# Gated attention's pieces spread over its blocks, the first loads on two queues, and the last normalization shared by VectorE and TensorE

## The chip, the cores and the metric

The kernel runs on one core of a Trainium2 chip. The metric is the device time of one execution in microseconds (us); a kernel is run several times and the median is compared. Everything below is about the five engines of that core: PE (TensorE, matmuls), DVE (VectorE), ACT (ScalarE), POOL (GpSimd) and SP (SyncE, which here only issues transfers), and about the core's 16 DMA engines.

## What is computed

One decoder layer over 256 tokens of 2048 features, in float32. Cut to what matters:

```
u = x @ W_in                                   # blocks cg, ca, v, qk, r, cq, ck, cv, sc, sh, sb of 512 columns, and g_low of 16
y_a = silu(LN(depthwise_conv31(ca * sigmoid(cg))))           # 31 taps over 256 tokens
log_a = log_sigmoid(g_low @ w_g2 + b_g2) / 16                # forget gate of the gated linear attention
y_b = rms_norm(chunked gated linear attention of q, k, v with exp(cumsum(log_a))) * silu(r)
y_c = dilated attention of cq, ck, cv;   y_d = sb * conv3(sc * sh)
x1  = LN1(alpha * x + (concat(y_a, y_b, y_c, y_d) * mix_scale) @ W_out)
acc = alpha * x1 + HierMoE(x1)                 # 32 experts, 2 for each token
      + sigmoid(x1 @ W_g + b_g) * (p @ W_p)
out = (acc - mean) * rstd * ln2_g + ln2_b      # LN2, the last normalization
```

## The kernel before

**Projections.** Each block of W_in is a [2048 x 512] weight that arrives in two halves of 8 row tiles (`k`). A call of `proj_ch` or `proj_tok` walks over the 16 `k`: ACT casts the weight tile to a rounded copy (`wh`, L252), DVE or POOL subtracts it from the original for the rest (`wl`, L255; every third tile goes to POOL), and PE multiplies three times: high by high, low by high, high by low (L275 to L277). That makes 12 matmuls of 256 columns for one `k`. Four pairs of `wh` and `wl` exist, so the split can run at most four tiles ahead of PE.

**The first block.** `first_half` loads weight and input in turn; `load_x` issues the transfer of some tiles of x, casts them (`xh`, L204) and subtracts (`xl`, L205). The first tile of x comes over SP's queue, the other eight transfers over POOL's; the weights `cgw` all come over SP's.

**The pieces.** After each `k` the projection calls `pump(rate)`. It runs `rate` pieces of work from the list `tasks` (generators, each piece up to a `yield`), and when `tasks` is empty from `behind`, which holds the 31-tap convolution `conv` of block A (DVE: 4 x 30 multiply-adds at L334). `gla_gate` (the forget gate) is the task under block `qk`, `gla_state` (the chunked state, 7 steps of four DVE updates between matmuls) under block `r`, `gla_out` under `cq`. `drain()` finishes what is left of `tasks`. On top of this order in the program, a scheduler of the framework orders the instructions of each engine, so the order in the program and that on an engine are not the same.

**Experts.** After routing, `group` runs ten groups of experts. Their weights stream over SP's queue into five slots; four expert units share the PE array in strips of 32 columns (L1101, L1144), and `scatter` adds the results to `acc` (L1161 to L1166). A spill-over path for overfull experts sits in a branch (`tc.If(flag > 0)`), not taken here; `flag` is computed on DVE (`ov`) and loaded into a register on every engine (L1214).

**The last normalization.** `norm_stats` (L665 to L673) gives mean, `rstd` and `-mean * rstd` for each token. The 256 x 2048 result is eight pieces of 128 x 512 (`rows(acc, t, db)`). Two of them (i = 1 and 4) go over ACT (L1229) and two POOL operations (L1230, L1231), six over two DVE operations each (L1237, L1239); each piece is written out by one transfer on SP's queue.

Of the kernel before, what the change touches and what calls it, by code (L numbers as in the profile page):

```python
# [19 lines left out]
P = 128  # L20
T = 256
# [103 lines left out]
def trunk(ctx, tc, where, vecs_d, lasting, early, gla, xT, x, pT_d, w_in, w_out, ple_w_gate, exp_w_gu, exp_w_down, ple_w_proj, out):  # L125
# [74 lines left out]
    xl = bx.tile([P, KT, T], F32R, name="xl", tag="xb")  # L200

    def load_x(ks):
        (nc.gpsimd if ks.start else nc.sync).dma_start(xin[:, ks], xT[:, ks])
        S.copy(xh[:, ks], xin[:, ks])  # L204
        V.tensor_sub(xl[:, ks], xin[:, ks], f32(xh[:, ks]))  # L205

# [4 lines left out]
    def quarter(q, part, shape=None, name="mix"):  # L211
        return qm.tile(shape or [P, 4, T], F32 if shape else F32R, name=name, tag=f"q{q}{part}")
# [21 lines left out]
    def drain():  # L234
        while tasks:
            pump()

    def load_half(w, name, sizes=(4, 4), before=None):

        s = slot([P, 8, 512], name)  # L240
        a = 0
        for n in sizes:
            if before is not None:
                before(a, a + n)
            nc.sync.dma_start(s[:, a:a + n], w[:, a:a + n])
            a += n
        return s
# [8 lines left out]
        return wh, wl  # L256

    def first_half(k, w, name):
        s = load_half(w, name, (2, 2, 2, 2) if k else (1, 1, 2, 2, 2), lambda a, b: load_x(slice(k + a, k + b)))
        if k:  # L260
            small_loads()
        return s
# [51 lines left out]
    wgl = const("wgl", t=at_g).rearrange("p (k c) -> p k c", k=KT)

    b = bank("gl")
    for k in range(KT):
        o = 32 * (k % 4)
        PE.matmul(b[o:o + 32, :T], wgl[:, k, :], xin[:, k, :], start=k < 4, stop=k >= KT - 4, skip_group_check=True,
                  tile_position=(0, o))  # L320
    glT = quarter(3, "l", [P, T], "glT")
    V.tensor_copy(glT, b[:, :T])
# [59 lines left out]
    behind.append(conv())  # L382


    vb = proj_tok(w_in[list(BLOCKS).index("v")], "v", lambda k: xh[:, k], lambda k: xl[:, k])
    vv = work([P, 2, 512], name="vv")
    for t in range(NT):
# [44 lines left out]
        yield  # L432

    tasks.append(gla_gate())
    us = proj_ch("qk")
    drain()
    qq = work([P, 2, 2, T], name="qq")
    kk = work([P, 2, 2, T], name="kk")
    for blk in range(2):
        V.scalar_tensor_tensor(qq[:, 0, blk, :], us[blk], 0.125, e12[:, 0, blk, :], op0=ALU.mult, op1=ALU.mult)  # L440
        V.scalar_tensor_tensor(qq[:, 1, blk, :], us[blk], 0.125, e34[:, 0, blk, :], op0=ALU.mult, op1=ALU.mult)
        V.tensor_mul(kk[:, 0, blk, :], us[2 + blk], e12[:, 1, blk, :])
        V.tensor_mul(kk[:, 1, blk, :], us[2 + blk], e34[:, 1, blk, :])

    ob = []

    def gla_state():
        kd = work([P, 2, 256], name="kd")
        state = work([P, 2, 2, 256], name="state")
        G.memset(state, 0.0)  # L450
# [52 lines left out]
            yield  # L503

    tasks.append(gla_state())
    rb = proj_ch("r")
    drain()
    sr = work([P, 4, T], name="sr")
    cg = cp.tile([P, 4], F32, name="cg")
# [45 lines left out]
    q_ = work([P, 4, T], name="q_")  # L555
    for cb in range(4):
        S.activation(q_[:, cb, :], backwards(cq[cb]), AF.Copy, scale=0.125)
    ck = proj_ch("ck")
    k_ = work([P, 4, T], name="k_")
    for cb in range(4):  # L560
        S.copy(k_[:, cb, :], ck[cb])
    cv = proj_tok(w_in[list(BLOCKS).index("cv")], "cv", lambda k: xh[:, k], lambda k: xl[:, k])
    v_ = work([P, 2, 512], name="v_")
    for t in range(NT):
        S.copy(v_[:, t, :], cv[t])
# [437 lines left out]
    def slots_and_gates():  # L1003
        for src, dst in ((sg4, sB), (gt.rearrange("p c t o -> p (c t o)"), gB)):
# [203 lines left out]
    ov = stage([1, 34], F32, name="ov")
    V.tensor_copy(ov[:, 0:32], orders[:, 32:64])
    V.tensor_sub(ov[:, 0:32], ov[:, 0:32], const("tab", 1)[:, 32:64])  # L1210
    V.reduce_max(ov[:, 32:33], ov[:, 0:32], axis=AX.X)
    V.tensor_scalar(ov[:, 32:33], ov[:, 32:33], 0.0, 1.0, op0=ALU.max, op1=ALU.min)
    V.tensor_copy(orders[:, 64:65], ov[:, 32:33])
    flag = nc.values_load(orders[0:1, 64:65], min_val=0, max_val=1, skip_runtime_bounds_check_because="0 or 1")  # L1214
# [5 lines left out]


    S.activation(agg[:, 8], eps_ln, AF.Sqrt)
    with tc.manual_schedule(engines={ET.DVE, ET.Pool, ET.Activation}):
        ms = norm_stats(4)
        for i in range(8):
            t, db = i % 2, i // 2
            if i in (1, 4):
                av = rows(acc, t, db)
                S.activation(av, av, AF.Identity, scale=ms[t][1], bias=ms[t][2])  # L1229
                G.tensor_mul(av, av, rows(gbB, 0, db))  # L1230
                G.tensor_add(av, av, rows(gbB, 1, db))  # L1231
                nc.sync.dma_start(out[t * P:(t + 1) * P, db * 512:(db + 1) * 512], av)
        todo = [i for i in range(8) if i not in (1, 4)]
        for js in ([0, 1], [2, 3], [4, 5]):
            part = [(rows(acc, i % 2, i // 2), i % 2, i // 2) for i in (todo[j] for j in js)]
            for av, t, db in part:
                V.scalar_tensor_tensor(av, av, ms[t][0], rows(gbB, 0, db), op0=ALU.subtract, op1=ALU.mult)  # L1237
            for av, t, db in part:
                V.scalar_tensor_tensor(av, av, ms[t][1], rows(gbB, 1, db), op0=ALU.mult, op1=ALU.add)  # L1239
                nc.sync.dma_start(out[t * P:(t + 1) * P, db * 512:(db + 1) * 512], av)  # L1240


# [22 lines left out]
```

## Time and profile before

| | |
|---|---|
| median of 3 runs | 958.7 us (956.8 to 960.71) |
| the profiled execution: its own time | 958.87 us |
| its span in the trace | 957.0 us |
| PE busy | 897.9 us (94% of the span) |
| DVE busy | 448.8 us (47%) |
| ACT busy | 294.9 us (31%) |
| POOL busy | 137.6 us (14%) |
| mean granted clock of PE | 0.983 of full speed |

The span is the time from the first to the last instruction; the execution's own time is 1.9 us longer. "Busy" of an engine is an average over stages in which different things end last, so it does not say what a change in one stage is worth. The stages are, roughly: the first block to 40 us, the other projections to 400 us, routing to 440 us, the experts to 936 us, and the last normalization.

### The profile page before, as it was taken

Reading aid. Unit: us, or ns where it says so; the run is one execution under the profiler, and the core shown is the slowest. Engines: PE = TensorE matmul, PEld = TensorE weight load, DVE = VectorE, ACT = ScalarE, POOL = GpSimd, SP = SyncE. Lnnn points to the kernel's source line nnn. Section 1 sums busy time; section 2 is a strip of 40 time slices with the busy share of each in tenths; the row PEclk is TensorE's granted clock in tenths of the full one; section 3 lists DMA queues with packets and bytes.
Section 4 is the critical chain, followed back from the end, with each engine's and each line's share of the span. In section 5 each row is a group of like instructions: output and inputs, shape, how many; then the busy total and the mean of one; then the engine's idle time right before and its main releaser. Section 6 shows DMA issues by size and latency. Waiting matters only on the chain. (4 is left out here: it accounts for less than half of the span.)

```text
span 957.0 us, 14896 instructions
## 1 busy us (share of the span) xinstructions
PE 897.9 (94%) x5542; PEld 546.9 (57%) x5542; DVE 448.8 (47%) x902; ACT 294.9 (31%) x537; POOL 137.6 (14%) x124
## 2 busy tenths in 40 slices
PE   8998899999999999989999989999999999998981
PEld 7897887998989888944333353234533342441220
DVE  4469999746558554563351051032403253340327
ACT  5444523557554544551110121011202121120012
POOL 3233322322322332200000000000000000000002
PEclk9999999999999999989999999999999999999996
DMA  9954422654444754329999999999999999999972
GB/s 343 420 194 175 164 102 94 222 188 158 177 177 174 252 196 176 132 80 351 385 369 409 403 400 410 401 407 416 407 407 396 415 417 417 409 407 394 338 269 90
DMA packets 75855, 280.88 MB, mean 293 GB/s; under 512 B 7000, under 2 KB 7136, under 8 KB 63744
## 3 DMA queue, kind: packets, MB, share of 16 engines
q1 hardware_dynamic: 72256, 267.40, 72.9%
q0 software_dynamic: 3520, 12.47, 3.3%
q8 instruction: 45, 0.74, 0.3%
q14 instruction: 34, 0.28, 0.1%
HBM read 290.31 MB, written 2.11 MB: 306 GB/s over the span
## 5 line engine op out<-in xcount | busy, mean ns | idle before, releaser
L1101 PE MATMUL gu<-we,xg 128*32 128x512 f32 x1184 | 157.7, 597 | 8.3 <-DMA we<-in_exp_w_gu_dram 8.3
L746 PE MATMUL pl<-plw,x1T 128*128 128x512 f32 x256 | 124.3, 618 | 0.0
L1101 PEld LDWEIGHTS gu<-we,xg 128*32 128x32 f32 x1184 | 37.6, 109 | 109.1 <-issue 74.5
L1144 PE MATMUL y<-wd,hT 128*32 128x512 f32 x624 | 84.8, 605 | 6.6 <-DMA wd<-in_exp_w_down_dram 3.6
L1126 DVE SCALAR_TENSOR_TENSOR h<-h,gw,gu 128x256 f32<-128x256 f32 x10 | 4.8, 482 | 180.7 <-ACT h L1125 180.7
L1164 DVE TENSOR_TENSOR xn<-xn,sc 128x512 f32<-128x512 f32 x76 | 50.5, 684 | 79.4 <-PE sc L1162 79.4
L746 PEld LDWEIGHTS pl<-plw,x1T 128*128 128x128 f32 x256 | 46.3, 193 | 67.7 <-issue 66.2
L1125 ACT ACTIVATE h<-gu 128x256 f32<-128x256 f32 x10 | 3.8, 384 | 220.1 <-PE gu L1101 220.1
L334 DVE SCALAR_TENSOR_TENSOR ya<-hp,ce,ya 128x255 f32<-128x255 f32 (+29 forms) x120 | 65.0, 587 | 0.2
L252 ACT CAST wh<-wow 128x512 fp32r<-128x512 f32 (+1 forms) x80 | 42.8, 535 | 46.6 <-PE wo L295 32.7
L1148 ACT CAST yh<-y 128x512 fp32r<-128x512 f32 x40 | 23.4, 586 | 106.0 <-PE sc L1161 60.0
L295 PE MATMUL wo<-wh,mix 128*128 128x512 f32 (+1 forms) x160 | 54.1, 347 | 0.0
L294 PE MATMUL wo<-wh,mix 128*128 128x512 f32 (+1 forms) x160 | 54.1, 347 | 0.0
L255 DVE TENSOR_TENSOR wl<-wow,wh 128x512 fp32r<-128x512 f32 (+1 forms) x53 | 32.2, 612 | 45.5 <-ACT wh L252 42.0
L723 POOL DMA_DIRECT2D plw<-in_ple_w_gate_dram x16 | 8.6, 534 | 279.0 <-PE pl L746 175.8
L1144 PEld LDWEIGHTS y<-wd,hT 128*32 128x32 f32 x624 | 18.0, 110 | 53.4 <-issue 28.9
L965 PE MATMUL xg<-M,xnh 128*128 128x256 f32 x160 | 43.6, 307 | 5.1 <-ACT xg L970 2.7
L1149 DVE TENSOR_TENSOR yl<-y,yh 128x512 fp32r<-128x512 f32 x40 | 27.4, 686 | 39.6 <-ACT yh L1148 39.0
L296 PE MATMUL wo<-wl,mix 128*128 128x512 f32 (+1 forms) x160 | 42.6, 347 | 0.0
L970 ACT ACTIVATE xg<-xg,cl 128x256 f32<-128x256 f32 x40 | 22.5, 564 | 59.5 <-DVE xg L973 59.5
L965 PE MATMUL xg<-M,xnl 128*128 128x256 f32 x160 | 39.9, 283 | 0.0
L965 PEld LDWEIGHTS xg<-M,xnh 128*128 128x128 f32 x160 | 30.4, 190 | 14.7 <-ACT xg L970 6.0
(481 smaller groups left out, 1942.2 us busy)
## 6 DMA issues: line engine op xcount, KB each, us to landing
we<-in_exp_w_gu_dram SPq DMA_DIRECT2D x168, 512.0 KB, 10.2
wd<-in_exp_w_down_dram SPq DMA_DIRECT2D x92, 512.0 KB, 10.8
we<-in_exp_w_gu_dram SPq DMA_DIRECT2D x32, 1024.0 KB, 15.8
wow<-in_w_out_dram SPq DMA_DIRECT2D x16, 1024.0 KB, 7.2
wd<-in_exp_w_down_dram SPq DMA_DIRECT2D x16, 1024.0 KB, 17.1
wd<-in_exp_w_gu_dram SPq DMA_DIRECT2D x24, 512.0 KB, 6.2
plw<-in_ple_w_gate_dram POOLq DMA_DIRECT2D x16, 512.0 KB, 7.0
plw<-in_ple_w_gate_dram SPq DMA_DIRECT2D x6, 1024.0 KB, 6.4
```

Source lines behind the costliest of these rows:

```text
L252: S.copy(wh, w)
L255: e.tensor_sub(wl, w, f32(wh))
L294: PE.matmul(o, lh(k)[:, ts], wh, start=i == 0, stop=False)
L295: PE.matmul(o, ll(k)[:, ts], wh, start=False, stop=False)
L296: PE.matmul(o, lh(k)[:, ts], wl, start=False, stop=i == KT - 1)
L334: V.scalar_tensor_tensor(ya[:, cb, d:T], hp[:, cb, 0:T - d], dww(30 - d, cb), ya[:, cb, d:T], op0=ALU.mult, op1=ALU.add)
L746: PE.matmul(bs[t], x1T[:, k, t * P:(t + 1) * P], s, start=False, stop=k == KT - 1, skip_group_check=True)
L965: PE.matmul(o, part[:, t, (k0 + j) * P:(k0 + j + 1) * P], m_[:, t, :], start=j + t + i == 0, stop=t + i == 2, skip_group_check=True)
L1101: PE.matmul(gu[us, :], xg[:, k0 + k, xo + us.start:xo + us.stop], s[:, q, k, :], start=k0 + k == 0, stop=k0 + k == KT - 1, skip_group_chec ...
L1144: PE.matmul(y[us, :], hT[:, k, us], s[:, q, k, c0:c0 + 512], start=k == 0, stop=k == 1, skip_group_check=True, tile_position=(0, us.start))
L1149: V.tensor_sub(yl, y, f32(yh))
L1164: V.tensor_add(rows(acc, t, db), rows(acc, t, db), o)
```

## The change

1. **First loads.** The first two tiles of x are issued by ACT, the rest by SP; POOL issues none. The pieces are larger: weights of the first half in 1, 1, 2 and 4 tiles (before 1, 1, 2, 2, 2), of the second half in 4 and 4 (before four of 2).
2. **Pieces.** The small projection of `g_low` (`wgl`, 16 matmuls) stands behind block `ca` and the start of the convolution instead of ahead of `ca`. The rates of `pump` become 0.6 under `qk`, 1.15 under `r`, and 1.25 under `ck` and `cv` (before 1 each). The eight operations that make `qq` and `kk` move from a block of their own into the first two pieces of `gla_state`.
3. **Flag.** `ov` is computed right after routing, and the flag is loaded before the last expert group.
4. **Last normalization.** POOL is out. DVE subtracts the mean and multiplies by `ln2_g` in all eight pieces. For i = 0 to 3, PE then adds `ln2_b` (`spread`: one matmul that spreads a row over 128 partitions) and multiplies by `rstd` with a diagonal matrix `dg` (one float32 matmul of 512 columns), and ACT copies the result out of PSUM. For i = 4 to 7 DVE does the second step too.

```
     def load_x(ks):
-        (nc.gpsimd if ks.start else nc.sync).dma_start(xin[:, ks], xT[:, ks])
+        (nc.scalar if ks.stop <= 2 else nc.sync).dma_start(xin[:, ks], xT[:, ks])
...
-        s = load_half(w, name, (2, 2, 2, 2) if k else (1, 1, 2, 2, 2), lambda a, b: load_x(slice(k + a, k + b)))
+        s = load_half(w, name, (4, 4) if k else (1, 1, 2, 4), lambda a, b: load_x(slice(k + a, k + b)))
...
-    us = proj_ch("qk")
+    us = proj_ch("qk", 0.6)
     drain()
-    qq = work([P, 2, 2, T], name="qq")
...
     def gla_state():
+        qq = work([P, 2, 2, T], name="qq")
+        kk = work([P, 2, 2, T], name="kk")
+        for blk in range(2):
+            V.scalar_tensor_tensor(qq[:, 0, blk, :], us[blk], 0.125, e12[:, 0, blk, :], op0=ALU.mult, op1=ALU.mult)
...
+            yield
...
-    rb = proj_ch("r")
+    rb = proj_ch("r", 1.15)
...
+            flag = nc.values_load(orders[0:1, 64:65], min_val=0, max_val=1, skip_runtime_bounds_check_because="0 or 1")
         group(g, RT[g], last=g == NG - 1)
...
+    with tc.manual_schedule(engines={ET.PE, ET.DVE, ET.Activation}):
         ms = norm_stats(4)
+        dg = []
+        for t in range(NT):
+            dg.append(stage([P, P], F32, name="dg"))
+            S.activation(dg[t], ident, AF.Identity, scale=ms[t][1])
+
         for i in range(8):
             t, db = i % 2, i // 2
...
+            av = rows(acc, t, db)
+            V.scalar_tensor_tensor(av, av, ms[t][0], rows(gbB, 0, db), op0=ALU.subtract, op1=ALU.mult)
+            if i < 4:
+                b = bank("o", "y", 3)
+                spread(b, 16 + db, True, False)
+                PE.matmul(b, dg[t], av, start=False, stop=True, skip_group_check=True)
+                S.copy(av, b)
+            else:
                 V.scalar_tensor_tensor(av, av, ms[t][1], rows(gbB, 1, db), op0=ALU.mult, op1=ALU.add)
+            nc.sync.dma_start(out[t * P:(t + 1) * P, db * 512:(db + 1) * 512], av)
```

**Where the instructions move: the start.** On SP's queue, the first rows of before are these (`xin` is x, `cgw` the first block's weight, the numbers are partitions by elements; `cl` and `cg__84` are small constants):

```order
L203 DMA xin<-in_xT_dram 128x256
L245 DMA cgw<-in_w_in_dram 128x512 x2
L245 DMA cgw<-in_w_in_dram 128x1024 x7
L184 DMA cl<-in_lasting_dram 128x670
L185 DMA cg__84<-in_gla_dram 128x776
```

and of the changed kernel these:

```order
L204 DMA xin<-in_xT_dram 128x512
L246 DMA cgw<-in_w_in_dram 128x512 x2
L246 DMA cgw<-in_w_in_dram 128x1024
L204 DMA xin<-in_xT_dram 128x1024
L246 DMA cgw<-in_w_in_dram 128x2048
L204 DMA xin<-in_xT_dram 128x1024
L246 DMA cgw<-in_w_in_dram 128x2048
L204 DMA xin<-in_xT_dram 128x1024
L246 DMA cgw<-in_w_in_dram 128x2048
L184 DMA cl<-in_lasting_dram 128x670
```

The tiles 2 and 3 of x now stand ahead of the first weight, and the rest of x stands between the weights in the order in which PE needs it; before, it came over another queue.

**The middle: DVE under block `r`.** Between the second and the fifth weight subtraction of block `r` (`wl<-rw`), before has these rows (`ya<-hp` is one multiply-add of the convolution):

```order
L440 SCALAR_TENSOR_TENSOR qq<-qk_910,e_907 128x256
L441 SCALAR_TENSOR_TENSOR qq<-qk_910,e_908 128x256
L442 TENSOR_TENSOR kk<-qk_911,e_907 128x256
L334 SCALAR_TENSOR_TENSOR ya<-hp,ce,ya 128x239
L255 TENSOR_TENSOR wl<-rw,wh 128x512
L334 SCALAR_TENSOR_TENSOR ya<-hp,ce,ya 128x239
L443 TENSOR_TENSOR kk<-qk_911,e_908 128x256
L442 TENSOR_TENSOR kk<-qk_911,e_907 128x256
L334 SCALAR_TENSOR_TENSOR ya<-hp,ce,ya 128x238
L443 TENSOR_TENSOR kk<-qk_911,e_908 128x256
L334 SCALAR_TENSOR_TENSOR ya<-hp,ce,ya 128x238
L255 TENSOR_TENSOR wl<-rw,wh 128x512 x2
```

and the changed kernel these, behind the same four `qq` and one `kk`:

```order
L325 SCALAR_TENSOR_TENSOR ya<-hp,ce,ya 128x239
L447 TENSOR_TENSOR kk<-qk_899,e_896 128x256
L446 TENSOR_TENSOR kk<-qk_899,e_895 128x256
L447 TENSOR_TENSOR kk<-qk_899,e_896 128x256
L325 SCALAR_TENSOR_TENSOR ya<-hp,ce,ya 128x239 x2
L256 TENSOR_TENSOR wl<-rw,wh 128x512
L325 SCALAR_TENSOR_TENSOR ya<-hp,ce,ya 128x238
L256 TENSOR_TENSOR wl<-rw,wh 128x512
L325 SCALAR_TENSOR_TENSOR ya<-hp,ce,ya 128x238
L256 TENSOR_TENSOR wl<-rw,wh 128x512
```

The third `wl` has moved behind three `kk` and two multiply-adds of the convolution, and the fourth and fifth follow it closer; up to the fifth the sum is the same but for one multiply-add. The scheduler has also kept the convolution at the same place overall: up to the last `wl` of `qk` DVE has 64 of its multiply-adds behind it in both kernels.

**The end.** On PE the program before has nothing behind the branch; the changed one has these rows (`pick` and `vecs` make the spread row, `dg` is the diagonal):

```order
L1171 MATMUL sc<-yl,MT 128x512
L1217 UNCONDITIONAL_BRANCH x2
L732 MATMUL o<-vecs,pick 128x512
L1239 MATMUL o<-xn,dg 128x512
L732 MATMUL o<-vecs,pick 128x512
L1239 MATMUL o<-xn,dg 128x512
```

and two more such pairs. On SP's queue the eight writes of the changed kernel wait for ACT (pieces 0 to 3) and DVE (4 to 7) in this order:

```order
L1243 DMA out_dram<-xn 128x512 [waits DMAHW2_49,Activation_49]
L1243 DMA out_dram<-xn 128x512 [waits DMAHW3_49,DVE_49]
L1243 DMA out_dram<-xn 128x512 [waits DMAHW4_49,Activation_49]
L1243 DMA out_dram<-xn 128x512 [waits DMAHW5_49,DVE_49]
L1243 DMA out_dram<-xn 128x512 [waits DMAHW6_49,DVE_49]
L1243 DMA out_dram<-xn 128x512 [waits DMAHW7_49,Activation_49]
L1243 DMA out_dram<-xn 128x512 [waits DMAHW0_49,DVE_49]
L1243 DMA out_dram<-xn 128x512 [waits DMAHW1_49,Activation_49]
```

So the last write is that of PE's and ACT's fourth piece; before, it was a piece of DVE. The register load of the flag has moved on PE and SP only: on DVE and ACT it still stands behind their last operation of the last group, ahead of the branch.

## Rows read from the trace of the kernel before

**Rows 1.** Two stretches: length, busy time by engine, granted PE clock, DMA share, GB/s.

```profile
100.00:120.00 20.00, 16.76 (x134) 15.83 (x133) 20.00 (x34) 10.14 (x17) 7.80 (x6) 1.00 0.55 202
...
860.00:880.00 20.00, 16.21 (x65) 3.20 (x64) 0.48 (x1) 1.34 (x3) 0.00 (x0) 1.00 1.04 396
```

**Rows 2.** Timeline of the start on ACT and PE; brackets: idle before, its releaser.

```profile
5.30 0.62 ACT L252 CAST wh<-cgw 128x512 fp32r<-128x512 f32 x1 [1.96 <-DMA cgw<-in_w_in_dram]
...
9.66 1.14 ACT L252 CAST wh<-cgw 128x512 fp32r<-128x512 f32 x2 [2.64 <-DMA cgw<-in_w_in_dram]
...
11.37 0.50 PE L275 MATMUL cg<-xh,wh 128*128 128x256 f32 x2 [0.68 <-ACT xh L204]
...
12.85 0.66 PE L276 MATMUL cg<-xl,wh 128*128 128x256 f32 x2 [0.97 <-DVE xl L205]
```

**Rows 3.** Stretches of the start, columns as in rows 1.

```profile
0.00:5.30 5.30, 3.79 (x16) 3.49 (x16) 0.61 (x4) 1.89 (x3) 4.25 (x12) 1.00 0.55 150
...
0.00:7.50 7.50, 5.31 (x23) 5.02 (x24) 2.08 (x7) 3.50 (x6) 4.62 (x12) 1.00 0.67 208
0.00:9.60 9.60, 7.41 (x33) 7.12 (x34) 2.33 (x7) 3.50 (x6) 4.62 (x12) 1.00 0.75 248
0.00:11.50 11.50, 8.63 (x41) 8.14 (x42) 2.99 (x8) 5.16 (x9) 5.76 (x13) 1.00 0.80 275
...
13.00:16.30 3.30, 3.30 (x17) 3.30 (x18) 2.44 (x3) 1.97 (x4) 1.28 (x1) 0.50 1.02 397
16.30:20.00 3.70, 3.70 (x32) 3.70 (x32) 1.42 (x3) 1.24 (x2) 0.73 (x1) 0.98 1.03 409
```

**Rows 4.** Waits of PE between 62 and 140 us: total, times, longest.

```profile
PE qk L277 <- DVE wl L255: 3.6, 4, 1.2
PE r L277 <- DVE wl L255: 1.7, 2, 1.2
PE v L296 <- DVE wl L255: 0.5, 1, 0.5
```

**Rows 5.** Groups on DVE, 62 to 140 us: busy, mean ns, idle before.

```profile
L334 DVE SCALAR_TENSOR_TENSOR ya<-hp,ce,ya 128x255 f32<-128x255 f32 (+22 forms) x90 | 50.6, 609 | 0.0
```

**Rows 6.** Timeline of the end on DVE, POOL and SP's queue.

```profile
934.79 2.59 DVE L1059 BATCH_NORM_STATS2 stat<-sum 128x6 f32<-128x512 f32 x4
...
940.20 0.39 DVE L665 BATCH_NORM_AGGREGATE agg<-stat 128x2 f32<-128x24 f32 x2 [2.81 <-DVEq L1215]
...
942.93 1.52 POOL L1230 TENSOR_TENSOR xn<-xn,gbB 128x512 f32<-128x512 f32 x1 [241.60 <-ACT xn L1229]
...
953.34 0.99 SPq L1240 DMA_DIRECT2D out_dram<-xn  x2
```

**Rows 7.** The chain that ended last, in order of time: start, length, what.

```profile
942.00 1.33 DVE xn L1237 x2
943.33 3.34 DVE xn L1239 x2
946.67 3.33 DVE xn L1237 x2
...
952.65 0.66 DVE xn L1239
```

**Rows 8.** Two stretches of PE: length, busy time, granted clock, DMA share, GB/s.

```profile
422.80:429.20 6.40, 6.04 (x10) 0.50 0.67 220
...
940.00:957.00 17.00, 0.00 (x0) 0.50 0.33 124
```

**Rows 9.** Prices: float32 matmul (425 to 429 us), spread row, PSUM copy, PE's register load.

```profile
L746 PE MATMUL pl<-plw,x1T 128*128 128x512 f32 x6 | 5.5, 1084 | 0.0
...
L731 PE MATMUL bg<-vecs,pick x8: 393/491/498, 736.8 to 858.1; 64*128 64x512 f32 x8
...
L1166 ACT COPY xn<-sum 128x512 f32<-128x512 f32 x4 | 2.1, 589 | 0.6 <-PE sum L1162 0.5
...
L1214 PEldq TENSOR_LOAD <-orders x1: 490/490/490, 934.9 to 934.9; - x1
```

More of the change, by code (lines that the diff above doesn't have):

```diff
@@ L313, in trunk @@
         S.activation(sg[:, cb, :], gate[cb], AF.Sigmoid)
[L314 to L322, printed above, removed]
     au = proj_ch("ca")
@@ L382, in trunk @@
     behind.append(conv())
+    wgl = const("wgl", t=at_g).rearrange("p (k c) -> p k c", k=KT)
+    b = bank("gl")
+    for k in range(KT):
+        o = 32 * (k % 4)
+        PE.matmul(b[o:o + 32, :T], wgl[:, k, :], xin[:, k, :], start=k < 4, stop=k >= KT - 4, skip_group_check=True,
+                  tile_position=(0, o))
+    glT = quarter(3, "l", [P, T], "glT")
+    V.tensor_copy(glT, b[:, :T])
     vb = proj_tok(w_in[list(BLOCKS).index("v")], "v", lambda k: xh[:, k], lambda k: xl[:, k])
@@ L434, in trunk @@
     tasks.append(gla_gate())
-    us = proj_ch("qk")
+    us = proj_ch("qk", 0.6)
     drain()
-    qq = work([P, 2, 2, T], name="qq")
[L438 to L443, printed above, removed]
     ob = []
     def gla_state():
+        qq = work([P, 2, 2, T], name="qq")
+        kk = work([P, 2, 2, T], name="kk")
+        for blk in range(2):
+            V.scalar_tensor_tensor(qq[:, 0, blk, :], us[blk], 0.125, e12[:, 0, blk, :], op0=ALU.mult, op1=ALU.mult)
+            V.scalar_tensor_tensor(qq[:, 1, blk, :], us[blk], 0.125, e34[:, 0, blk, :], op0=ALU.mult, op1=ALU.mult)
+            V.tensor_mul(kk[:, 0, blk, :], us[2 + blk], e12[:, 1, blk, :])
+            V.tensor_mul(kk[:, 1, blk, :], us[2 + blk], e34[:, 1, blk, :])
+            yield
         kd = work([P, 2, 256], name="kd")
@@ L557, in trunk @@
         S.activation(q_[:, cb, :], backwards(cq[cb]), AF.Copy, scale=0.125)
-    ck = proj_ch("ck")
+    ck = proj_ch("ck", 1.25)
     k_ = work([P, 4, T], name="k_")
@@ L561, in trunk @@
         S.copy(k_[:, cb, :], ck[cb])
-    cv = proj_tok(w_in[list(BLOCKS).index("cv")], "cv", lambda k: xh[:, k], lambda k: xl[:, k])
+    cv = proj_tok(w_in[list(BLOCKS).index("cv")], "cv", lambda k: xh[:, k], lambda k: xl[:, k], 1.25)
     v_ = work([P, 2, 512], name="v_")
@@ L1010, in slots_and_gates @@
             yield
+    ov = stage([1, 34], F32, name="ov")
+    V.tensor_copy(ov[:, 0:32], orders[:, 32:64])
+    V.tensor_sub(ov[:, 0:32], ov[:, 0:32], const("tab", 1)[:, 32:64])
+    V.reduce_max(ov[:, 32:33], ov[:, 0:32], axis=AX.X)
+    V.tensor_scalar(ov[:, 32:33], ov[:, 32:33], 0.0, 1.0, op0=ALU.max, op1=ALU.min)
+    V.tensor_copy(orders[:, 64:65], ov[:, 32:33])
     def start_sum():
@@ L1205, in trunk @@
     man.close()
[L1208 to L1214, printed above, removed]
     with tc.If(flag > 0):
@@ L1222, in trunk @@
     S.activation(agg[:, 8], eps_ln, AF.Sqrt)
-    with tc.manual_schedule(engines={ET.DVE, ET.Pool, ET.Activation}):
+    with tc.manual_schedule(engines={ET.PE, ET.DVE, ET.Activation}):
         ms = norm_stats(4)
+        dg = []
+        for t in range(NT):
+            dg.append(stage([P, P], F32, name="dg"))
+            S.activation(dg[t], ident, AF.Identity, scale=ms[t][1])
         for i in range(8):
             t, db = i % 2, i // 2
[L1227 to L1238, printed above, removed]
+            av = rows(acc, t, db)
[6 more added lines that the diff above has]
+            else:
                 V.scalar_tensor_tensor(av, av, ms[t][1], rows(gbB, 1, db), op0=ALU.mult, op1=ALU.add)
-                nc.sync.dma_start(out[t * P:(t + 1) * P, db * 512:(db + 1) * 512], av)
+            nc.sync.dma_start(out[t * P:(t + 1) * P, db * 512:(db + 1) * 512], av)
 _OUTS = [((1, T, D), 'float32')]
```

## Prediction

> **What bounds the kernel now.** I read the stretches of the span first, then PE's waits, then the timelines of the start and the end. Between 40 and 400 us PE is full nearly everywhere; the gap is around 100 us, where DVE is busy all 20 of 20 us and PE only 16.76 [rows 1]. In the experts the DMA engines are full while PE idles (860 to 880 us: DMA share 1.04, PE 16.21 of 20) [rows 1]: there only bytes count. So a saving ahead of the experts moves their whole stream forward, and one at the end comes off the end; one in the engines' work during the experts is worth nothing. The change touches three places: the start, the DVE-bound blocks `v`, `qk` and `r`, and the tail behind the last matmul.
>
> **The start.** The first weight lands at 5.30 us, those for k = 2 and 3 only at 9.66, and ACT, which takes things in order, idles 2.64 us for them [rows 2]. Then it casts those two weights before x's tiles 2 and 3, so PE waits 0.68 us for `xh` and 0.97 for `xl` [rows 2], and from 13.0 to 16.3 us it runs at half its clock [rows 3]. The bytes say why the weights are late. By 5.3 us 150 GB/s moved 0.80 MB; SP's queue up to the first weight holds 0.13 + 0.26 = 0.39 MB. By 9.6 us 2.38 MB had moved; SP's queue up to k = 3 holds 1.18 MB. Both times it is half: the tiles of x on POOL's queue take every second byte, also for k = 4 to 15, which nobody needs yet [rows 2, 3].
>
> In the changed kernel all but 0.26 MB (on ACT's queue) lies in one queue in the order of need. I take the same bytes by the same time. Up to the first weight: 0.26 (tiles 2 and 3 of x) + 0.26 + ACT's 0.26 = 0.79 MB, so 5.3 us as now: no gain in PE's first matmul. Up to k = 3: 1.57 MB, which had moved by 7.5 us (208 GB/s) instead of 9.6 [rows 3]. k = 4 to 7 come as one transfer, all at once: 3.15 MB, so 11.5 us (275 GB/s) [rows 3], 12.1 after a cast of 0.62 [rows 2]. PE needs k = 4 after 48 matmuls: at full clock they start 0.116 us apart (32 in 3.7 us), at half clock 0.19 (17 in 3.3) [rows 3], so between 11.5 and 15 us; PE did start at half pace, so I take no wait. Then the two waits go (1.65 us), and with them the half clock of 3.3 us, which costs half of itself (1.65): **-3.3 us**. Bounds: 0 (another wait in their place), and -4.3 if the first weight also comes 1 us sooner without POOL's queue. ACT pays two issues, covered by its idle time up to 5.30; two issues of 0.5 us each (as SP pays, 0.99 for two) [rows 6] end before x is there. The projection of `g_low` is the same 16 matmuls later, and x's slot is held until they are done; with five slots and DMA at half load (share 0.55 [rows 1]) I price that at nothing; without that cover it is one late half weight in `r`.
>
> **The middle.** PE waits 3.6 + 1.7 + 0.5 = 5.8 us for `wl` on DVE [rows 4]. DVE's filler is the convolution: 90 multiply-adds of 0.56 us (50.6 us) in 78 us [rows 5]. The rates move pieces in the program, but what DVE gets is the scheduler's order, and there the change is small: 64 multiply-adds ahead of the last `wl` of `qk` in both kernels. Under `r` the third `wl` stands behind three `kk` and two multiply-adds more than before (I estimate 2 us, at 0.56 or less each), and those after it follow at once, so up to the fifth nothing is lost or won but one multiply-add. Elsewhere in `qk` and `r` single multiply-adds have moved across a `wl`, some ahead of it and some behind; each that PE no longer waits for is worth 0.56 us. I take one of them net, **-0.6 us**, between +2 (the third `wl` waited for in full) and -5.8 (all waits gone).
>
> **The flag.** On DVE the register load stays where it was, between the last BN statistics (ending at 937.4) and 940.20; so does the gap of 2.81 us [rows 6]: 0. PE's load takes 0.49 us [rows 9] and now stands ahead of the last group's matmuls; it is covered there by PE's waits for weights, 3.8 us of idle time in 860 to 880 us [rows 1]; uncovered it costs 0.5. The five small `ov` operations on DVE move from the experts to behind routing, with PE on other work: 0, at most 0.8 us if PE waited for all of them.
>
> **The tail.** Now DVE's 12 operations run from 942.00 to 953.31; of six pairs four take 1.33 us and two 3.33, and the two lie where POOL works [rows 6, 7]. Without POOL: 12 x 0.665 = 8.0 us, so DVE ends at 950.0. Behind it is PE and ACT's half. The trace has PE at half clock from 940 to 957 us, idle since 936 [rows 8], so it starts slow. The nearest row at that clock is the float32 matmul of 512 columns at 425 to 429 us: 6 records in 5.5 us, two for one matmul, so 1.84 us [rows 9]. The spread row is one fp32r matmul of 512 columns, 0.39 us as a record at full clock [rows 9]; 0.43 apart at half (estimate: 256 columns start 0.19 to 0.21 apart). DVE's first piece is ready at 942.7: matmuls end at 944.6, 946.8, 949.1, 951.4; ACT's copy takes 0.53 (four in 2.1) [rows 9], so the fourth piece is ready at 952.0. But PE's clock comes back under steady work: after routing the half clock lasted 6.4 us [rows 8], at the start 3.3 [rows 3]. If it returns between 946 and 949, the fourth piece is ready at 949.4 to 950.7, beside DVE's last at 950.0.
>
> The last write is now issued behind that. Before, the last piece was ready at 953.31 and, with a write ahead of it in the queue, issued at about 953.9, 3.1 us ahead of the span's end. So I take 950.0 to 950.7, plus up to 0.4 for the write ahead, plus 3.1: 953.6 to 954.2, against 957.0: **-3.1 us**; -1.9 if PE stays slow to the end, -3.4 if it is fast at once.
>
> **Sum.** -3.3 - 0.6 - 3.1 = -7.0 on the profiled execution's 958.87: 951.9. That execution lies 0.2 above the median of the runs shown, 958.7, so 951.7 us, -0.73%. A measurement here can tell about 0.5%, 4.8 us, from no change: faster means below 953.9.
>
> **Rivals.**
> - *The start gains nothing* (15%). The first weights stand behind tiles of x that PE doesn't need first, and k = 4 to 7 come as one large transfer; if the first cast or k = 4 is 2 us late, PE idles again and the half clock returns. Against it speak the byte counts, exact at both points. Time: 951.7 + 3.3 = 955.0. A sentence of the Trainium skill speaks for this rival (Trainium Kernel Development and Optimization, Key Constraints): transfers issued from SP, ACT and POOL all run on the same 16 engines and interleave, and issuing from several only saves issue time. By that, moving x between queues would win no bandwidth; the trace agrees on the interleaving (half and half), but what I count on is order, which the sentence leaves open.
> - *The middle pays in full* (8%): the spread pieces take all 5.8 us out. Against it: DVE is still full, 20 of 20 us, and its order has hardly moved. 951.7 - 5.2 = 946.5.
> - *PE paces the tail at half clock* (10%): the fourth piece at 952.0 gives -1.9 in place of -3.1: 952.9. For it: PE's only work is one matmul chain after 6 us of idling. The skill has the half clock as the default state that activity lifts (TensorE: Matmul & The Clock Gate, Part 1); by it both outcomes are possible here.
> - *Slower: the state's steps hold PE* (5%). `gla_state` has seven steps in which PE's matmul waits for DVE's update, and all of `r` queues behind it. If the moved `qq` and `kk` push each update behind a further group of four multiply-adds (4 x 0.56 = 2.2 us), that is up to 15 us; from 1 us a step it eats the whole gain, and at 2 us a step the time is 951.7 + 14 = 966. Against: PE shows no wait for the state now.
>
> **Chances.** Forecast 62%, the rivals 38% as given. The likeliest case's own range is 949.5 to 953.9. Leaving out the slower rival, the full middle and the far ends of the first leaves 948.5 to 956.0. Faster: forecast, middle, slow tail and a little less for the combinations, 0.71; same: the first rival, and slow tail with a weak start, 0.24; slower 0.05.
>
> **What would show it.** The cast of k = 2 at about 7.5 us and no half clock between 10 and 20 us; the end of block `cg` 3 us earlier. PE's waits for `wl` from 62 to 140 us between 4 and 6 us. In the tail, pairs of DVE all at 1.33 us, float32 matmuls of `o` at 1.84 us first and 0.97 later, ACT's fourth copy by 951. The forecast is wrong if the experts' stream does not begin some 4 us sooner than now, or if the last write is issued after 952.

## The result and the profile after

The changed kernel takes 952.5 us (median of 9 runs, 949.89 to 954.98); the kernel before, on the same chip, 958.55 us (9 runs, 956.8 to 960.71). The ratio is 0.9937, 95% interval 0.9925 to 0.9949: 6.0 us less, where 951.7 us was forecast. The sum came out nearly right, but not its terms: the start gained more than forecast, the last normalization about half, and the middle nothing.

The profiled execution of the changed kernel is its fastest one (949.89 us, span 948.0), so 8.98 us below the profiled one of before; some 3 us of that are not the change: against the medians it is 6.0, and the table below the experiments shows where the rest lies.

**The start.** ACT's timeline, where [rows 2] had the first weight at 5.30 us and that of k = 2 at 9.66:

```profile
4.63 0.92 ACT L205 CAST xh<-xin 128x512 fp32r<-128x512 f32 x2 [1.47 <-DMA xin<-in_xT_dram]
5.89 0.62 ACT L253 CAST wh<-cgw 128x512 fp32r<-128x512 f32 x1 [0.34 <-DMA cgw<-in_w_in_dram]
...
8.20 1.14 ACT L253 CAST wh<-cgw 128x512 fp32r<-128x512 f32 x2 [0.86 <-DMA cgw<-in_w_in_dram]
9.47 1.05 ACT L205 CAST xh<-xin 128x1024 fp32r<-128x1024 f32 x1
12.07 1.14 ACT L253 CAST wh<-cgw 128x512 fp32r<-128x512 f32 x2 [1.55 <-DMA cgw<-in_w_in_dram]
```

The first weight comes 0.6 us later than before, k = 2 and 3 come 1.5 us sooner, and from 6.56 us on PE waits for nothing up to 40 us. Three stretches, with the columns of [rows 3]:

```profile
0.00:7.50 7.50, 4.72 (x20) 4.43 (x21) 2.17 (x8) 3.85 (x7) 0.20 (x4) 1.00 0.74 228
...
13.00:16.30 3.30, 3.30 (x30) 3.30 (x30) 2.95 (x4) 2.67 (x5) 1.29 (x1) 1.00 1.02 420
16.30:20.00 3.70, 3.70 (x33) 3.70 (x33) 2.25 (x4) 2.43 (x5) 1.49 (x1) 1.00 0.99 397
```

Between 13 and 16.3 us stand 30 matmuls at a clock of 1.00, where before there were 17 at 0.50 [rows 3]. Block `ca` is done (first `hp` on DVE) at 56.8 us, before at 62.2.

**The middle.** PE's waits from 57 to 135 us, the waits of [rows 4]:

```profile
PE qk L278 <- DVE wl L256: 2.2, 3, 1.2
PE qk L278 <- DVE cm L416: 1.5, 1, 1.5
PE r L278 <- DVE wl L256: 1.1, 1, 1.1
PE kdt L469 <- issue: 0.3, 1, 0.3
```

The waits for `wl` fell from 5.8 to 3.3 us, and a new one of 1.5 us (for `cm` of the forget gate) took most of it back: 5.1 us of waits in all. DVE is as full as before:

```profile
100.00:120.00 20.00, 17.44 (x140) 16.11 (x141) 20.00 (x41) 9.76 (x17) 5.16 (x4) 1.00 0.32 117
```

**The end.** Timeline of DVE, PE, ACT and SP's queue behind the last matmul of the experts, to set beside [rows 6, 7]:

```profile
927.28 2.59 DVE L1068 BATCH_NORM_STATS2 stat<-sum 128x6 f32<-128x512 f32 x4
...
932.69 0.38 DVE L666 BATCH_NORM_AGGREGATE agg<-stat 128x2 f32<-128x24 f32 x2 [2.82 <-DVEq L1217]
...
934.41 3.40 DVE L1235 SCALAR_TENSOR_TENSOR xn<-xn,agg,gbB 128x512 f32<-128x512 f32 x5
...
935.31 2.04 PE L1239 MATMUL o<-xn,dg 128*128 128x512 f32 x2 [1.80 <-DVE xn L1235]
...
937.28 0.79 PE L732 MATMUL o<-vecs,pick 64*128 64x512 f32 x1
...
938.01 2.07 PE L1239 MATMUL o<-xn,dg 128*128 128x512 f32 x2
...
942.20 0.75 DVE L1242 SCALAR_TENSOR_TENSOR xn<-xn,agg,gbB 128x512 f32<-128x512 f32 x1
...
942.90 1.13 PE L1239 MATMUL o<-xn,dg 128*128 128x512 f32 x2
944.06 0.59 ACT L1240 COPY xn<-o 128x512 f32<-128x512 f32 x1 [0.90 <-PE o L1239]
```

PE starts a piece every 2.7 us (935.31, 938.01): 1.97 for the float32 matmul and 0.73 for the spread row. DVE is done at 942.95; PE's and ACT's fourth piece only at 944.65. The stretches show why:

```profile
930.00:932.00 2.00, 0.00 (x0) 0.00 (x0) 0.00 (x0) 0.77 (x1) 0.00 (x0) 0.97 0.06 16
932.00:942.00 10.00, 7.45 (x9) 2.35 (x9) 8.76 (x19) 2.07 (x5) 0.00 (x0) 0.50 0.19 70
942.00:944.00 2.00, 2.00 (x4) 0.48 (x3) 0.92 (x2) 0.59 (x1) 0.00 (x0) 0.97 0.84 311
```

PE has 0.50 of its clock (1.2 GHz) until 942 us; only the fourth piece runs at 2.4 GHz. From the start of the last four BN statistics to the end of the span it is 20.7 us, before 22.2 [rows 6].

### The profile page after: what moved, and what is told of

Read it like the earlier page. It is cut to its first block, busy times and chain, and to the rows that moved or that the text cites. A ratio compares the mean times of both kernels' runs of the same rounds, so it can differ in the third digit from the quotient of the medians.

```text
span 948.0 us, 14907 instructions
## 1 busy us (share of the span) xinstructions
PE 902.9 (95%) x5554; PEld 547.9 (58%) x5554; DVE 442.0 (47%) x899; ACT 295.8 (31%) x538; POOL 126.9 (13%) x112
## 6 DMA issues: line engine op xcount, KB each, us to landing
we<-in_exp_w_gu_dram SPq DMA_DIRECT2D x168, 512.0 KB, 10.2
wd<-in_exp_w_down_dram SPq DMA_DIRECT2D x92, 512.0 KB, 10.7
wd<-in_exp_w_gu_dram SPq DMA_DIRECT2D x24, 512.0 KB, 5.1
plw<-in_ple_w_gate_dram POOLq DMA_DIRECT2D x16, 512.0 KB, 6.9
```

## Experiments

Line numbers differ by a few between kernels. A difference in us that stands with a ratio is worked out from the ratio; the medians by themselves give 4.8, 0.4, 0.8 and 0.5 us less for experiments 1 to 4. The table behind the last experiment sets all profiles side by side.

**1. The first loads alone.** Only this part of the change on the kernel before:

```
-        (nc.gpsimd if ks.start else nc.sync).dma_start(xin[:, ks], xT[:, ks])
+        (nc.scalar if ks.stop <= 2 else nc.sync).dma_start(xin[:, ks], xT[:, ks])
...
-        s = load_half(w, name, (2, 2, 2, 2) if k else (1, 1, 2, 2, 2), ...
+        s = load_half(w, name, (4, 4) if k else (1, 1, 2, 4), ...
```

> Only the first loads are changed; the small projection of g_low stays ahead of block ca. Theory: the first loads carry most of the gain. In the profile of the whole change block ca ends 5.4 us sooner, about 1 us of which is the 16 matmuls of g_low that stand later there; so here ca ends 4 to 5 us sooner than before, no half clock between 10 and 20 us, and the time falls by 4 to 5 us (ratio 0.995 to 0.996). Rival A, the sum of the prediction: 3.3 us (0.9966). Rival B, that a start made faster is given back before the experts (by DVE, or by late weights): ca ends sooner, the time stays within 1 us.

Measured: 953.54 us, ratio 0.9945 (0.9926 to 0.9964), 5.3 us less. `ca` ends at 57.9 us, 4.3 sooner, although the first matmul starts at 6.92, 0.95 later. There is no half clock in the granted clock and no wait of PE behind that for the first weight. One gain was not in the forecast: the small matmuls of `g_low` (32 records) stood in four batches between those of `cg` and `ca`, and stand in one here. Groups on PE from 0 to 64 us, busy and mean ns, of before and then of this kernel:

```profile
L319 PE MATMUL gl<-xin,cg__84 128*32 128x256 f32 x32 | 3.4, 386 | 0.0
```

```profile
L320 PE MATMUL gl<-xin,cg__84 128*32 128x256 f32 x32 | 1.9, 382 | 0.0
```

That is 1.5 us, and the same from start to start on PE. In the whole change they stand in several batches (2.8 us busy), and 26 of the 32 still run ahead of the end of `ca`, not behind it as the expectation has it. The theory stands; that the gain is given back before the experts does not.

**2. The middle alone.** `g_low` behind `ca`, the rates of the pieces, `qq` and `kk` inside `gla_state`:

```
+    us = proj_ch("qk", 0.6)
+    rb = proj_ch("r", 1.15)
...
+    ck = proj_ch("ck", 1.25)
```

> Only the middle is changed: g_low moved behind block ca, the rates of the pieces, qq and kk inside the state's pieces. Theory: DVE is full in these blocks and its order hardly moves, so the time stays within 1 us of before (0.999 to 1.001); the end of sh stands where it was within 1 us. Rival A: the pieces do take PE's waits for wl out, up to 5.8 us (0.994). Rival B: the state's steps come later and PE waits for them: slower by 1 to 3 us, with the waits of block r grown by that.

Measured: 957.91 us, ratio 0.9998 (0.9983 to 1.0013). The profiled execution shows the old start at its worst, `ca` done at 67.7 us, so places are compared from there on. Counted from the end of `ca`, the last matmul of `qk` comes 1.2 us sooner than before (+52.2 in place of +53.4), that of `r` 1.1 later (+91.1 for +90.0), of `cq` 0.7 sooner, of `sh` 0.4 later, and of `wo` (the output projection) 0.4 later (+337.5 for +337.1). The 1.2 us are no gain: the four matmuls `z` of the forget gate stand ahead of the end of `ca` here and behind it before. Behind the new start, with `z` where it was, the same middle ends `qk` 0.4 us sooner, `r` 1.9 and `wo` 1.1 us later than before, alike in four kernels. Block `r` ends later because the state's last step (4 more records of `ob` and 8 of `upd`, 2.3 us of PE's time) runs under it and no longer under `cq`, which ends level again; under `sh` about 1 us more is lost, and why isn't shown. The theory (nothing within 1 us) holds; a full gain of 5.8 us does not.

**3. The last normalization alone.** The last part of the diff on the kernel before:

> Only the last normalization is changed. Theory: PE paces it at half clock: about 2.7 us for a spread row with its float32 matmul, first piece 2.9 us behind the mean, fourth copy some 10.3 us behind DVE's first operation where the last piece of before was 11.3 us behind it: 1.0 to 1.9 us less (0.998 to 0.999). Rival: the prediction's 3.1 us (0.9967), with the clock back between the second and the third piece.

Measured: 957.53 us, ratio 0.9984 (0.997 to 0.9998), 1.5 us less. From the last four BN statistics (935.3) to the end of the span (956.3) it is 21.0 us, PE's pieces again 2.7 us apart at a clock of 0.50 until 950 us. The theory stands.

**4. The flag alone.** `ov` behind routing, the load of the flag ahead of the last group:

> Only the flag is moved: ov behind routing, its load ahead of the last expert group. Theory: DVE and ACT still load it behind their last operation, so the gap of 2.8 us ahead of the last normalization stays and the time stays within 0.5 us (0.9995 to 1.0005). Rival: the profile of the whole change shows 1.1 us lost between block sh and the end of routing; if the ov operations on DVE do that, it shows here as 1 us more.

Measured: 957.82 us, ratio 0.9998 (0.9986 to 1.0009), and routing as late behind `ca` as in before. The term of 0 stands; the rival falls.

**5. Matmuls that keep PE awake in the tail.** On the changed kernel:

```
     second_moments()
+    awake("gu", 15)     # matmuls of 128 columns into a bank that nobody reads
     man.close()
...
+        awake("gu", 18)
         ms = norm_stats(4)
```

> The changed kernel, with 15 matmuls that nobody reads behind the last scatter and 18 more between the branch and the last normalization, so that PE does not idle long there. Theory: the tail's remaining loss is PE's clock, granted at 0.50 from 932 to 942 us. With PE at 1.00 a spread row and its float32 matmul take about 1.4 us together in place of 2.7, the fourth copy ends some 3 us sooner, and DVE's last operation (8.5 us behind its first) becomes the end: from the start of the last four BN statistics to the end of the span 19.0 us in place of 20.7, 1.7 us less than the changed kernel. Rival: the copies out of PSUM and the waits between spread and matmul set the pace, not the clock: pieces still 2.4 us or more apart, less than 0.5 us gained.

Measured: 951.67 us, ratio 0.9937 (0.992 to 0.9954), no gain over the changed kernel. The mechanism is right and the dose wrong. Timeline of PE and of SP's queue:

```profile
934.14 4.25 PE L1206 MATMUL awake<-ones 128*128 128x128 f32 x36 [1.71 <-DVE agg L667]
...
938.33 0.50 PE L732 MATMUL o<-vecs,pick 64*128 64x512 f32 x1
...
938.75 1.12 PE L1246 MATMUL o<-xn,dg 128*128 128x512 f32 x2
939.81 0.50 PE L732 MATMUL o<-vecs,pick 64*128 64x512 f32 x1
...
940.53 5.75 SPq L1250 DMA_DIRECT2D out_dram<-xn  x8
```

The clock is 1.00 throughout, and a piece takes 1.48 us (938.33, 939.81). But the 18 matmuls (0.24 us each) hold PE until 938.3 with its first input ready at 935.9, and SP's queue, in order, holds DVE's finished pieces behind PE's: DVE is done at 943.80, ACT's fourth copy at 944.95, and two of DVE's writes stand behind it, the last issued at 945.87. The eight issues are 0.72 us apart in the mean because they wait for the copies; back to back they are 0.42 to 0.48 apart.

**6. Without the branch.** The spill-over path for overfull experts and the load of the flag are left out of the changed kernel:

> The changed kernel without the branch: the spill-over path for overfull experts and the load of the flag are left out. Theory: the gap of 2.8 us ahead of the last normalization is the jump over that path, not the load of the flag, so no earlier load can take it away and the term of the flag had to be 0; without the branch DVE goes on at once: 2.8 to 3.5 us less than the changed kernel, 17 to 18 us from the last four BN statistics to the end of the span. Rival: the gap is the register load (0.55 us on DVE) and what queues behind it: 0.5 us less.

Measured: 951.4 us, ratio 0.9937 (0.9921 to 0.9952). The gap is gone: BN statistics from 928.5, aggregation between them at 930.55, end at 946.0, 17.5 us in place of 20.7. So the gap is the jump over the path; 2.65 of the 3.2 us lie ahead of DVE's first operation on `xn`, and the rest comes from PE's clock, which returned at 938 us here, 4.2 us behind PE's first piece in place of 6.8. The jump's rows in the changed kernel (duration, start):

```profile
L1217 PEldq COMPARE_BRANCH  x1: 3458/3458/3458, 927.4 to 927.4; - x1
L1217 ACTq COMPARE_BRANCH  x1: 45/45/45, 929.0 to 929.0; - x1
L1217 DVEq COMPARE_BRANCH  x1: 76/76/76, 929.7 to 929.7; - x1
...
L1217 DVEq EVENT_SEMAPHORE  x1: 21/21/21, 932.6 to 932.6; - x1
```

PE spends 3.46 us in it, DVE 2.9 up to the next thing that its queue does. The load of the flag, which this experiment leaves out too, is not the gap: on DVE the jump begins behind it. The DMA queues between 926 and 934 us show what the jump brings with it; in this experiment no packet moves there (queue, kind: packets, MB, share of the DMA engines):

```profile
q8 instruction: 2, 0.03, 1.5%
q14 instruction: 3, 0.02, 1.0%
```

The Trainium skill (Runtime: NRT & Kernel Launch, Instruction fetch mechanics) says that a taken branch to a place that has not been fetched ahead stalls the engine until its instructions come. The trace agrees with that for PE and DVE, and ACT, which goes on after 0.4 us, it does not explain. The time hardly moved, in part for another reason: without the branch the first spread row slipped ahead of six of the last group's matmuls and took one of their three banks, and ACT waited for `y` 3.29 us there in place of 1.91; the last BN statistics start 9.7 us behind the issue of the last weight transfer, not 8.0. So 3.2 us were won and about 1.7 lost in this profile. It is by 3 us the fastest of its six runs (947.95 us, the others 950.91 to 952.16); why the others gain nothing over the changed kernel isn't shown.

**7. The first weights ahead of x.** On the changed kernel, SP's queue in the order as written:

```
+        with tc.manual_schedule(engines={ET.SP}):
             s = load_half(w, name, (4, 4) if k else (1, 1, 2, 4), ...
```

> The changed kernel, with the order on SP's queue as written: the first two weights ahead of tiles 2 and 3 of x. Theory: the first matmul waits for the first weight, which in the changed kernel stands behind 0.26 MB of x and came 0.6 to 0.9 us later than before; here the first cast of a weight starts at about 5.2 us in place of 5.9 and block ca ends 0.5 to 1 us sooner; the time falls by that. Rival: bytes ahead don't set it, since few bytes move before 5 us anyway: the first cast stays at 5.8 to 6.2 us.

Measured: 950.94 us, ratio 0.9928 (0.9912 to 0.9944); `ca` done at 56.5 us in place of 56.8. The weight landed at 5.45 us in place of 5.87, and tile 0 of x on ACT's queue at 5.63 in place of 4.42, so that x became the late one:

```profile
5.65 0.40 ACT L205 CAST xh<-xin 128x256 fp32r<-128x256 f32 x1 [2.47 <-DMA xin<-in_xT_dram]
5.96 0.61 ACT L253 CAST wh<-cgw 128x512 fp32r<-128x512 f32 x1
```

The cast of the first weight starts at 5.96 us in place of 5.89, and PE's first matmul at 6.62 in place of 6.56, as the rival had it. The tail took 22.4 us in this profile, 1.7 more than in the changed kernel's with the same code: PE was at 0.50 until 944 us, and the fourth copy ended 18.4 us behind the start of the last BN statistics in place of 17.4. So 1.0 of the 1.7 us is when the clock comes back; the other 0.7 lies behind the fourth copy.

**8. The queue alone.** The kernel before with the new queues and the old, smaller pieces: the first two lines of experiment 1's diff.

> The kernel before with only the queue of x changed (tiles 0 and 1 from ACT, the rest from SP), the pieces as small as they were. Theory: what helps is that x and the weights stand in one queue in the order of need; the four profiles with the old start show PE waiting 1.7 to 4.6 us for tiles of x or weights between 9 and 25 us, the two with the new start none. So this alone gives most of the 5.3 us: 4 to 5.3 us, no wait of PE for x, block ca done before 59 us. Rival: the larger pieces (fewer issues on SP) are what helps: 2 us or less here.

Measured: 950.04 us, ratio 0.9924 (0.9908 to 0.994), 7.3 us less. PE's waits from 5 to 40 us in three profiles with the old start (experiments 2, 3 and 4), and then here:

```profile
PE cg L276 <- DVE xl L205: 4.6, 2, 3.6
...
```

```profile
PE gl L319 <- DMA cg__84<-in_gla_dram: 2.2, 1, 2.2
PE cg L275 <- ACT xh L204: 1.5, 1, 1.5
```

```profile
PE cg L275 <- ACT xh L204: 2.5, 1, 2.5
PE cg L276 <- DVE xl L205: 1.0, 1, 1.0
```

```profile
PE cg L275 <- ACT wh L252: 2.3, 1, 2.3
```

With the new queues only the wait ahead of the first matmul is left. So the queues give all of the start's gain, and the larger pieces none that shows (-7.3 without them, -5.3 with them; the intervals overlap). The theory stands. A rival isn't tested: the old queue was POOL's, which the profile lists as `software_dynamic` and SP's and ACT's as `hardware_dynamic`, and its eight issues take 4.4 us of POOL's time. No run keeps x on a queue of its own other than POOL's, so what order gives and what leaving POOL's queue gives aren't told apart.

**9. Awake at the start.** The kernel of experiment 8 with `keep_awake(15)` in place of `keep_awake(8)` (matmuls that nobody reads):

> The kernel before with the new queues of x, pieces as small as before, and 15 matmuls that nobody reads at the start in place of 8, so that PE is busy from 2.7 us until the first weight is there at 6.7. Theory: with the new queues what is left of the start is PE's slow pace: matmuls of block cg start 0.21 us apart from 6.9 to 11 us, 0.12 after that, although no wait is left. Kept busy from 2.7 us on, PE should be at 0.12 by 7.5 us: block ca done at 56 to 56.5 us in place of 57.8, the time 1 to 2 us below the kernel with the queues alone (ratio to before about 0.990 to 0.992). Rival: the slow pace comes from the start of the program whatever PE does: ca done at 57.5 to 58, no gain.

Measured: 950.56 us, ratio 0.9924 (0.9907 to 0.994): as without. Yet in the profile the mechanism works; PE's timeline at the start:

```profile
6.80 0.40 PE L276 MATMUL cg<-xl,wh 128*128 128x256 f32 x2
7.19 0.39 PE L277 MATMUL cg<-xh,wl 128*128 128x256 f32 x1
7.42 0.28 PE L275 MATMUL cg<-xh,wh 128*128 128x256 f32 x1
7.53 0.28 PE L276 MATMUL cg<-xl,wh 128*128 128x256 f32 x1
```

They start 0.12 apart almost from the start on. In experiment 8 they began so too, but fell back to 0.21 with the granted clock, from 7.6 to 11 us (columns as before):

```profile
7.60:11.00 3.40, 3.40 (x17) 3.38 (x17) 2.50 (x4) 2.35 (x5) 1.28 (x1) 0.50 1.03 409
```

`ca` is done at 56.2 in place of 57.8, and routing also 1.6 us sooner. In the experts of this profile that is lost (table).

**10. The queue, and a tail that is kept awake.** The kernel of experiment 8 with the changed flag and last normalization, 8 and 9 matmuls around the branch, and the writes in the order in which pieces come ready:

```
+        for i in (0, 1, 4, 2, 5, 3, 6, 7):
+            nc.sync.dma_start(out[t * P:(t + 1) * P, db * 512:(db + 1) * 512], rows(acc, t, db))
```

> The kernel before with the new queues of x (small pieces), the flag loaded early and the changed last normalization, in which 8 matmuls that nobody reads stand ahead of the branch and 9 behind it, and the writes stand in the order in which the pieces come ready (0, 1, 4, 2, 5, 3, 6, 7). Theory: PE stays at full clock, spread and float32 matmul take 1.5 us a piece from 935.3 on the scale of the changed kernel's profile, PE's fourth copy ends ahead of DVE's last operation, and DVE paces the end: 18.8 to 19.3 us from the start of the last four BN statistics to the end of the span (changed kernel 20.7, before 22.2). The time is 7.3 + 3 = 10 us below before (0.9895). Rival: the writes set the end, as where 33 matmuls were added and the eight writes were issued 0.72 us apart: 20 us or more.

Measured: 947.13 us, ratio 0.9884 (0.9866 to 0.9901), 11 us less than before: the fastest of all. The tail takes 18.9 us (927.9 to 946.8), as the theory had it:

```profile
936.10 1.12 PE L1245 MATMUL o<-xn,dg 128*128 128x512 f32 x2
937.15 0.49 PE L731 MATMUL o<-vecs,pick 64*128 64x512 f32 x1
...
941.70 0.59 ACT L1246 COPY xn<-o 128x512 f32<-128x512 f32 x1 [0.90 <-PE o L1245]
...
942.94 0.75 DVE L1248 SCALAR_TENSOR_TENSOR xn<-xn,agg,gbB 128x512 f32<-128x512 f32 x1
```

ACT's fourth copy now ends at 942.3, ahead of DVE's last operation.

**11. Both.** Experiments 9 and 10 together:

> Both: the kernel of the new queues with the awake start and the tail with a warm PE. Theory: the gains lie at two ends of the span and add: 1 to 2 us at the start and 3 at the end over the queues alone, 0.988 to 0.990. Rival: what is won ahead of the experts is lost in their stream, which ends on the DMA engines: no better than 0.9895.

Measured: 948.33 us, ratio 0.99 (0.9883 to 0.9918), no better than experiment 10. In the profile the tail took 20.3 us: PE's clock fell although the same matmuls were added (two stretches, columns as before),

```profile
932.00:934.00 2.00, 1.80 (x11) 1.83 (x12) 1.42 (x9) 0.36 (x2) 0.00 (x0) 0.68 0.02 4
934.00:936.00 2.00, 2.00 (x10) 1.77 (x9) 2.00 (x4) 0.54 (x2) 0.00 (x0) 0.50 0.00 0
```

and PE's pieces came late: ACT's fourth copy ends at 942.57, and DVE's last two writes, ready by 942.39, stand behind it in the queue, the last issued at 943.53.

**12. The writes on two queues.** Experiment 11, with ACT issuing its own four pieces:

```
                 S.copy(av, b)
+                nc.scalar.dma_start(out[t * P:(t + 1) * P, db * 512:(db + 1) * 512], av)
```

> The kernel with both additions, with the writes on two queues: ACT issues those of its four pieces right behind its copies, SP those of DVE's four. Theory: where both additions were made, PE's clock fell all the same, its first piece came late, and the pieces of DVE stood behind it in the one queue, so that eight issues of 0.72 us set the end (20.3 us from the last four BN statistics to the end of the span). With two queues the end is DVE's last operation again, whatever PE's clock: 18.8 to 19.2 us, and a ratio to before of 0.987 to 0.989. Rival: the writes themselves (eight of 0.26 MB) share the DMA engines and take as long from two queues: 20 us, 0.990.

Measured: 948.54 us, ratio 0.9897 (0.9881 to 0.9914). The tail is 18.9 us, as expected, but in this execution the clock was 1.00 all the way, so whether two queues help when it falls isn't shown. The ratio is a little above the range expected, which its interval reaches.

**All profiles side by side.** Microseconds from the profiles: end of `ca`, end of routing (the cast of `orders`), start of the last four BN statistics, end of the span.

| profile | `ca` | routing | last BN | end | routing to BN | BN to end |
|---|---|---|---|---|---|---|
| before | 62.2 | 422.2 | 934.8 | 957.0 | 512.6 | 22.2 |
| 1 first loads | 57.9 | 418.0 | 931.2 | 953.9 | 513.2 | 22.7 |
| 2 middle | 67.7 | 428.0 | 939.4 | 961.8 | 511.4 | 22.4 |
| 3 last normalization | 62.4 | 422.5 | 935.3 | 956.3 | 512.8 | 21.0 |
| 4 flag | 63.6 | 423.6 | 935.4 | 957.7 | 511.8 | 22.3 |
| whole change | 56.8 | 417.9 | 927.3 | 948.0 | 509.4 | 20.7 |
| 5 awake tail | 56.6 | 417.8 | 928.0 | 949.7 | 510.2 | 21.7 |
| 6 no branch | 56.4 | 417.6 | 928.5 | 946.0 | 510.9 | 17.5 |
| 7 weights first | 56.5 | 417.6 | 927.6 | 950.0 | 510.0 | 22.4 |
| 8 queue alone | 57.8 | 416.7 | 926.9 | 949.2 | 510.2 | 22.3 |
| 9 awake start | 56.2 | 415.1 | 927.1 | 949.4 | 512.0 | 22.3 |
| 10 queue and tail | 57.8 | 416.8 | 927.9 | 946.8 | 511.1 | 18.9 |
| 11 both | 56.0 | 414.9 | 926.7 | 947.0 | 511.8 | 20.3 |
| 12 two queues | 56.8 | 415.7 | 927.9 | 946.8 | 512.2 | 18.9 |

In experiments 2 and 8 to 12 the four matmuls of `z` (1.2 us) stand ahead of the end of `ca`, in the others behind it. The experts' stretch (routing to BN) varies by 3.8 us between profiles, more than some of the gains. All the three with an awake start need about 512 us; whether an earlier start always loses that much there, or three executions happened to be slow, stays open.

## Why the prediction came out as it did

**The start, -3.3: right mechanism, mis-sized.** k = 2 came at 8.20 us (forecast 7.5), the two waits and the half clock from 13 to 16.3 us went, as forecast. Alone it measured -5.3 us (-7.1 to -3.5), beyond the forecast's bound of -4.3 but not clear of it; with the smaller pieces -7.3 (-8.8 to -5.7), clear of it. Three things were missing. The forecast took the waits of one profile, 1.65 us, as their size; in the next three with the old start PE waits 3.5 to 4.7 us between 9 and 25 us for tiles of x, weights or the constants of `g_low`, so the old start varies and the profiled one was a good case. Packing `g_low`'s matmuls gave 1.5 us in experiments 1 and 8 and 0.6 in the whole change. Against that, the first matmul came 0.6 to 0.95 us later, where the byte count gave no difference. The rival that the start gains nothing falls. By the Trainium skill's sentence (Trainium Kernel Development and Optimization, Key Constraints) issuing from several queues saves only issue time. The bandwidth hardly rose (228 against 208 GB/s up to 7.5 us), which agrees; experiment 8 shows what the sentence leaves open: moving x between the queues was worth more than any other part. That the order of arrival does it is what the waits that went fit; it is argued, since no run tells it from leaving POOL's queue.

**The middle, -0.6: wrong sign in the profiles, nothing in the time.** The step "I take one multiply-add net" fell: `wl`'s waits went down by 2.5 us, but a wait of 1.5 us for `cm` came, and `wo` ends 0.4 to 1.1 us later. In the time it is nothing (0.9998, whose interval holds -0.6 too). The rival that the pieces take all 5.8 us out falls, and so does the slower one: PE idles 0.3 us ahead of a matmul of the state, and the 1.9 us by which `r` ends later are the last step's matmuls, which `cq` no longer has.

**The flag, 0: right** (0.9998), for the reason given and one more: the gap is the jump, which no earlier load shortens.

**The tail, -3.1: half of it.** It measured -1.5 (-2.9 to -0.2), as the rival that PE paces the tail at half clock had it (-1.9). The step that failed is "if its clock returns between 946 and 949": on that scale (7.5 us earlier in the changed profile, by the BN statistics) it returned only at 949.5 to 950. On that scale the last write is issued at 952.2, so the forecast's own sign against it (after 952) came true. The estimates were a little small too: spread row 0.73 us and not 0.43 (which is what it takes at a clock of 1.00: 0.42 in experiment 5), float32 matmul 1.97 and not 1.84, DVE's 12 operations 8.54 and not 8.0, since the alternating ones take 0.75 us each. And the forecast's own terms give 953.1 to 954.2 for the end, not 953.6 to 954.2. Experiment 10 shows the other side: with the clock at 1.00 (and the writes reordered) the tail is 18.9 us, 3.3 below the 22.2 of before, which is what the forecast gave for a PE that is fast at once (-3.4).

**The sum.** -5.3 - 0.2 - 0.2 - 1.5 = -7.2 from the parts, against -6.0 measured for the whole; the intervals of the parts (1.1 to 1.8 us either way) allow that. The profiles of before and after tell the same: the end of `ca` 5.4 us sooner, 1.1 of it lost by routing, and the tail 1.5 us shorter, 5.8 in all. The forecast of -7.0 met the time by luck: what it took too small at the start and too large in the middle and the tail nearly cancelled.

## What to carry to other kernels

Put first loads on few queues in the order of need, and judge a start by several executions, since its waits differ from one to the next. Before giving a short last step to PE, read the granted clock there: the same four pieces cost 2.7 us each at 0.50 and 1.48 at 1.00. A few idle matmuls, dosed so that they end as the input comes, can hold the clock (experiments 10 and 12), but did not in experiment 11. In a single in-order queue of writes, order them by when pieces come ready.

## What was not expected of the hardware

- The jump over the untaken path takes PE 3.46 us and DVE 2.9, ACT 0.4 (PE 3.4 to 3.9 in the other profiles). DVE's part of it sits on the path of the end in every kernel but experiment 6.
- At the start the clock column reads 1.00 while matmuls of 256 columns start 0.21 us apart, the pace of a stretch at 0.50. That 1.00 is no reading: the trace's records of the clock begin only where the slow pace ends, at 10.3 us in the changed kernel and at 12.7 in experiment 1. Where it ends differs between executions of the same start: with eight idle matmuls three of eleven profiles (experiments 3, 4 and 8) have the pace of 0.12 from the first matmuls of `cg` on, with fifteen all three (experiments 9, 11 and 12).
- With the same idle matmuls in the tail, PE idled 2.7 us around the jump in experiment 10 and kept a clock of 1.00, and 2.6 us in experiment 11 and fell to 0.50. What decides between them isn't shown here.
